# A one-core decoder layer: gated convolution pieces stored from ScalarE's queue one piece later, gates loaded two pieces ahead into five buffers

## The chip, the cores and the metric

The kernel runs on one core of one Trainium2 chip. The metric is the device time of one execution in microseconds; lower is better. The engines are named as in the profile: PE is TensorE (PEld its weight load), DVE is VectorE, ACT is ScalarE, POOL is GpSimd, SP is SyncE. SP, ACT and POOL have queues from which they start DMA transfers; each queue is worked through in its written order, so an instruction that waits holds what stands behind it. SBUF is the on-chip memory, PSUM the accumulators of PE, DRAM the chip's main memory.

## The reference

One decoder layer for a prompt of 2048 tokens and a sample group of 8 x 4 tokens. A normalised input is projected into eleven parts of 512 columns. Four groups of heads are computed from them, each is multiplied by its own gate, and the 2048 columns so made go through `w_out`, a norm and a residual sum:

```python
h = rms_norm(x, pre_g)
z = h @ w_in
y_c, conv_new = conv_branch(ca, cb, conv_hist, w_dw, b_dw, ln_g, ln_b, w_pw, b_pw)
y_p, pool_new = pool_branch(pu, pool_hist, pos, pool_w, pool_scale)
y_s = sb_fn(q, k, v, sb_bias)            # stick-breaking attention
y_m = mem_attend(mq, mk, mv)             # cross attention
mix = concatenate([y_c * silu(cg), y_p * silu(pg), y_s * silu(sg), y_m * silu(mg)])
out = rms_norm(mix @ w_out, post_g)
y = x + out
```

The change touches the end of the convolution branch, `y_c * silu(cg)`. The branch is a gated input, a depthwise convolution of width 31, and then

```python
y = silu(layer_norm(y, ln_g, ln_b))
y = y @ w_pw + b_pw                      # 512 x 512, the "pointwise" product
```

The data are fp32.

## The kernel before

**Stages.** Projections, sample work and the depthwise convolution come first, then the stick-breaking attention of the prompt up to about 1985 us, and then the out stage up to the end. The out stage holds the product `mix @ w_out` and, woven into its first part, the rest of the convolution branch (layer norm, silu, pointwise product, gate). The parts of `mix` go through DRAM: the four groups, as they are finished, are stored to `mixd` (prompt) and `mixs` (sample), and loaded again as the operands of the product.

**Products in fp32.** PE multiplies operands of type fp32r. Each operand is split in two: a rounded copy (`hi`, a cast on ACT) and what that leaves (`lo`, a subtraction on DVE); three matmuls (hi hi, hi lo, lo hi) make one product.

**The product with `w_out`** (L1548 to L1760) is done as seven smaller products over blocks of a 2 x 2 split, in the order 1, 7, 2, 6, 4, 5, 3. Operands are sums and differences of blocks. For a part of `mix`: `out_load` loads `mr` on SP (L1620 to L1644), `out_combine` adds or subtracts two of them on POOL (L1657, L1661) or DVE (L1660), `out_high` casts to `mh` on ACT (L1669), `out_low` makes `ml` on DVE (L1680), and `out_part` runs the matmuls (L1915), four steps of three to a part. Operands are prepared four parts ahead (`AHEAD = 4`). For a weight tile: SP loads `wor` (L1548 to L1560), POOL makes the sum (L1570), ACT casts it to `wohi` (L1576), DVE makes `wolo` (L1581). Sums that a later product needs as well are stored from SP to `wsd` (weights) and `msd` (parts), L1565, and loaded again later.

**The convolution branch here** (`conv_post`, L1388) runs over eight blocks of 256 tokens, named by their first token in buffer names (`cgt512_1` is the gate of block 512, piece 1); the last block also holds the 32 sample tokens. For one block:

- `load` brings `cy` (the convolved input) on SP (L1399), `total` sums its four groups of 128 channels on POOL (L1406), `center` multiplies by a matrix of ones on PE (L1411), subtracts the mean on DVE (L1414), squares on ACT (L1416) and sums on POOL (L1418).
- `scale` does the same product for the variance (`cv`, L1424), then a square root on ACT (L1425, with a table load of its own ahead of it), a reciprocal on DVE (L1426), the affine step on DVE (L1433), the sigmoid on ACT (L1436, with a table load again), the product on DVE (L1440), and the split into `shi` (ACT, L1442) and `slo` (DVE, L1445).
- `point` makes four pieces of 128 output channels. Each has twelve matmuls (L1466) into a PSUM bank `cz`; then DVE adds the bias and multiplies by the gate (L1469), writing over the gate's own tile `cgt`; then SP stores that tile to `mixd` (L1471; in the last block the sample part to `mixs`, L1473). Two steps of the product with `w_out` follow each piece. There are two such PSUM banks, which the `cz` and `cm` tiles take in turn, so a piece's matmuls wait for the gate multiply of an earlier one.
- The gates, silu(cg), were computed earlier and lie in DRAM (`gcd`). `gate(i, co)` loads one piece on SP (L1452) into one of three buffers. The first gate of a block is asked for at the block's start, each other one when the piece before it begins.

The next block's `center` comes ahead of a block's `point`, and the steps of its `scale` after it. The steps of `conv_post` are paced against those of the product (one for every 0.9, `OPACE`), so PE's order is set by the code. DVE, ACT, POOL and SP get theirs from a scheduler, which puts an instruction where it expects its inputs and buffers to be ready. `wq` in the code is SP's queue.

Of the kernel before, what the change touches and what calls it, by code (L numbers as in the profile page):

```python
# [8 lines left out]
F32 = mybir.dt.float32  # L9
# [9 lines left out]
P = 128  # L19
# [30 lines left out]
CB = 256  # L50
# [36 lines left out]
def kernel(  # L87
# [9 lines left out]
    pe, act, dve, pool, sp = nc.tensor, nc.scalar, nc.vector, nc.gpsimd, nc.sync  # L97
    wq = nc.sync
# [22 lines left out]
    gcd = dram.tile([4, P, SEQ + NS], F32, name="gcd")  # L121
# [4 lines left out]
    mixs = dram.tile([4, P, 4, NS], F32, name="mixs")  # L126

    def mix_rows(ct, t0, n):

        return mixd[ct // 4, t0 // P : (t0 + n) // P, :, ct % 4].rearrange("b p t -> p b t")  # L130

    def by_tile(t):
        return t.rearrange("p (b t) -> p b t", t=P)
# [1254 lines left out]
    def conv_post(cp, ps_, weights):  # L1388


        CW = CB + NS
        blocks = [(a, a + CB) for a in range(0, SEQ - CB, CB)] + [(SEQ - CB, SEQ + NS)]
        ys, sums, sqs, split, gates = {}, {}, {}, {}, {}
# [7 lines left out]
        def total(i):  # L1401
            if i < len(blocks):
                a0, N = blocks[i][0], blocks[i][1] - blocks[i][0]
                sums[i] = cp.tile([P, CW], F32, tag="cs", name=f"cs{a0}", bufs=1)[:, :N]
                for c in range(3):
                    pool.tensor_tensor(out=sums[i], in0=sums[i] if c else ys[i][:, 0, :N], in1=ys[i][:, c + 1, :N], op=ALU.add)  # L1406

        def center(i):
            a0, N, y = blocks[i][0], blocks[i][1] - blocks[i][0], ys[i]
            mps = ps_(f"cm{a0}")  # L1410
            pe.matmul(mps[:, :N], lhsT=ones_ln, rhs=sums.pop(i), start=True, stop=True)  # L1411
            sq = []
            for c in range(4):
                dve.tensor_tensor(out=y[:, c, :N], in0=y[:, c, :N], in1=mps[:, :N], op=ALU.subtract)  # L1414
                sq.append(cp.tile([P, CW], F32, tag="csq", name=f"csq{a0}_{c}", bufs=4)[:, :N])
                act.activation(out=sq[c], in_=y[:, c, :N], func=AF.Square)  # L1416
            for a, b in ((0, 1), (2, 3), (0, 2)):
                pool.tensor_tensor(out=sq[a], in0=sq[a], in1=sq[b], op=ALU.add)  # L1418
            sqs[i] = sq[0]

        def scale(i):
            a0, N, y = blocks[i][0], blocks[i][1] - blocks[i][0], ys.pop(i)
            vps = ps_(f"cv{a0}")
            pe.matmul(vps[:, :N], lhsT=ones_ln, rhs=sqs.pop(i), start=True, stop=True)  # L1424
            act.activation(out=vps[:, :N], in_=vps[:, :N], func=AF.Sqrt, bias=eps_t)  # L1425
            dve.reciprocal(out=vps[:, :N], in_=vps[:, :N])  # L1426
            yield
            shi, slo = [cpw.tile([P, 4, CW], F32R, tag=n, name=f"{n}{a0}", bufs=1) for n in ("shi", "slo")]
            for two in ((0, 1), (2, 3)):
                ts = {}  # L1430
                for c in two:
                    t = ps_(f"ct{a0}_{c}")[:, :N]
                    dve.scalar_tensor_tensor(out=t, in0=y[:, c, :N], scalar=par[:, c, CONV_K + 1 : CONV_K + 2],  # L1433
                                             in1=vps[:, :N], op0=ALU.mult, op1=ALU.mult)
                    sg = cp.tile([P, CW], F32, tag="csq", name=f"csg{a0}_{c}", bufs=4)[:, :N]
                    act.activation(out=sg, in_=t, func=AF.Sigmoid, bias=par[:, c, CONV_K + 2 : CONV_K + 3])  # L1436
                    ts[c] = t, sg
                yield
                for c, (t, sg) in ts.items():
                    dve.scalar_tensor_tensor(out=t, in0=t, scalar=par[:, c, CONV_K + 2 : CONV_K + 3], in1=sg,  # L1440
                                             op0=ALU.add, op1=ALU.mult)
                    act.copy(shi[:, c, :N], t)  # L1442
                yield
                for c, (t, _) in ts.items():
                    dve.tensor_tensor(out=slo[:, c, :N], in0=t, in1=shi[:, c, :N].bitcast(F32), op=ALU.subtract)  # L1445
            split[i] = shi, slo
            load(i + 2)

        def gate(i, co):
            a0, a1 = blocks[i]  # L1450
            gates[i, co] = cp.tile([P, CW], F32, tag="cgt", name=f"cgt{a0}_{co}", bufs=3)
            wq.dma_start(gates[i, co][:, : a1 - a0], gcd[co, :, a0:a1])  # L1452

        def point(i):
            a0, a1 = blocks[i]
            N = a1 - a0
            shi, slo = split.pop(i)
            for co in range(4):
                g = gates.pop((i, co))
                if co < 3:  # L1460
                    gate(i, co + 1)
                ps = ps_(f"cz{a0}_{co}")
                n = 0
                for c in range(4):
                    for w, x in ((whi, shi), (whi, slo), (wlo, shi)):
                        pe.matmul(ps[:, :N], lhsT=w[:, c, P * co : P * (co + 1)], rhs=x[:, c, :N], start=n == 0,  # L1466
                                  stop=n == 11)
                        n += 1
                dve.scalar_tensor_tensor(out=g[:, :N], in0=ps[:, :N], scalar=par[:, co, CONV_K + 3 : CONV_K + 4],  # L1469
                                         in1=g[:, :N], op0=ALU.add, op1=ALU.mult)  # L1470
                wq.dma_start(mix_rows(co, a0, CB), by_tile(g[:, :CB]))  # L1471
                if N > CB:
                    wq.dma_start(mixs[0, :, co], g[:, CB:N])  # L1473
                yield
                yield
            flags.add(("conv", i))

        load(0)
# [9 lines left out]
        cpw = weights()  # L1488
# [14 lines left out]
        for _ in range(4):  # L1503
            yield
        for i in range(len(blocks)):
            gate(i, 0)
            side = iter(())
            if i + 1 < len(blocks):
                center(i + 1)
                side = scale(i + 1)  # L1510
            for _ in range(D2):
                yield
            for _ in point(i):
                yield
            total(i + 2)
            for _ in side:
                yield
            for _ in range(D1):
                yield
# [354 lines left out]
    def side_work():  # L1874
        nonlocal opm, conv
        for i, part in enumerate((sample_mem, sample_end)):
            with tc.tile_pool(name=f"sm{i}", bufs=1, side="left", reuse_waits="tile") as sm2:
                yield from part(sm2, side_ps, S)
        opm = ox.enter_context(tc.tile_pool(name="opm", bufs=1, side="left", reuse_waits="tile"))
        yield from out_weights(1, opm, pool)  # L1880
        while (3, 0) not in flags:
            yield
        for x in lead_:
            out_load(x)
            out_combine(x)
            out_high(x)
            out_low(x, pool)
            yield

        while (3, 1) not in flags:  # L1890
            yield
        for x in parts[2 * LEAD : 2 * LEAD + 3]:
            out_load(x)
        cp = cx.enter_context(tc.tile_pool(name="cp", bufs=1, side="left", reuse_waits="tile"))
        conv = conv_post(cp, lambda n: conv_ps[0](n), lambda: cx.enter_context(
            tc.tile_pool(name="cpw", bufs=1, side="left", reuse_waits="tile")))
        while "centered" not in flags:
            next(conv)
            yield
# [130 lines left out]
    for n, x in enumerate(parts):  # L2030
# [8 lines left out]
        prod, i, h = x  # L2039
# [55 lines left out]
```

## Time and profile before

| | |
|---|---|
| median of 3 runs | 2420.67 us (2415.16 to 2429.53) |
| the profiled execution's own time | 2418.47 us |
| its span, first to last instruction | 2416.7 us |
| mean granted PE clock | 0.982 of full speed |
| DVE, ACT, POOL busy over the span | 71%, 46%, 54% |
| gate loads L1452, first to last | 1571.1 to 2208.5 us |
| gate multiplies L1469, first to last | 2012.2 to 2211.0 us |
| stores L1471, first to last | 2012.7 to 2211.5 us |

Profile rows give times in microseconds from the start of the span. A row of the timeline is start, duration, engine, line, operation, output and input, and in square brackets how long the engine had been idle before, with what ended that. A row of a group of instructions ("x46") gives their busy time, the mean duration of one in nanoseconds, the idle time before them in all and what ended it. A row of waits names the engine and line that waited, the engine and line waited for, and then microseconds in all, number of times and the longest. SPq is SP's DMA queue.

### The profile page before, as it was taken

How to read it: one execution, taken by the hardware profiler on the slowest of the kernel's cores; microseconds unless marked ns; L12 is line 12 of the kernel's file. 1: busy time of each engine (PE TensorE's matmuls, PEld its weight loads, DVE VectorE, ACT ScalarE, POOL GpSimd, SP SyncE). 2: the span in 40 equal slices, each digit the busy share in tenths (PEclk: the TensorE clock that was granted, in tenths of full speed). 3: DMA queues.
4: the chain of work that ended last, by engine and by line, in shares of the span. 5: the costliest groups of instructions: out<-in, count | busy, mean ns of one | idle time of the engine just before them, and what ended most of it. 6: DMA issues, size and time to landing. Idle time of an engine off the chain costs nothing. (4 is left out here: it accounts for less than half of the span.)

```text
span 2416.7 us, 42137 instructions
## 1 busy us (share of the span) xinstructions
PE 2285.6 (95%) x15962; PEld 1774.5 (73%) x15962; DVE 1718.3 (71%) x2410; ACT 1117.5 (46%) x1939; POOL 1306.8 (54%) x1333
## 2 busy tenths in 40 slices
PE   7999999999999999999999998899999998989897
PEld 6998978898888777777777776455555556768775
DVE  5333774959757664587877777879798846687998
ACT  5322343242442322124242434788989954443554
POOL 2554544556574555655556564667877755453430
PEclk9999999999999999999999999999999999999998
DMA  5789988887778899987887767834333227887764
GB/s 179 223 260 298 348 290 287 284 272 263 263 254 292 277 344 325 323 287 262 275 270 269 262 218 179 239 79 117 89 88 79 64 64 242 266 272 254 245 234 170
DMA packets 340437, 562.14 MB, mean 233 GB/s; under 512 B 28481, under 2 KB 212929, under 8 KB 323834
## 3 DMA queue, kind: packets, MB, share of 16 engines
q1 hardware_dynamic: 284858, 290.72, 39.2%
q0 software_dynamic: 55376, 268.72, 31.3%
q8 instruction: 126, 2.06, 0.3%
q14 instruction: 77, 0.63, 0.1%
HBM read 469.28 MB, written 90.68 MB: 232 GB/s over the span
## 5 line engine op out<-in xcount | busy, mean ns | idle before, releaser
L959 DVE STREAM_TRANSPOSE T<-kt 128x1024 f32<-128x1024 f32 x256 | 308.9, 1226 | 183.4 <-PE sSA L972 177.2
L926 POOL DMA_INDIRECT vt<-in_cache_v_dram,idv x256 | 251.6, 983 | 242.1 <-PE sO L1011 181.5
L617 DVE SCALAR_TENSOR_TENSOR cacc<-U,par,cacc 128x512 f32<-128x512 f32 x480 | 360.2, 750 | 11.8
L1311 POOL TENSOR_TENSOR be<-be,E 128x512 f32<-128x512 f32 (+2 forms) x320 | 303.8, 957 | 118.4 <-DVE E L1302 52.4
L1302 DVE TENSOR_TENSOR_SCAN E<-gam,cr,ZM 128x513 f32<-128x513 f32 x192 | 232.8, 1262 | 15.1 <-ACT gam L1287 14.2
L926 POOL DMA_INDIRECT kt<-in_cache_k_dram,idk x128 | 126.2, 986 | 201.9 <-DVE T L959 146.8
L1322 PEld LDWEIGHTS AT<-ident,be 128*128 128x128 f32 x1088 | 117.7, 142 | 127.6 <-ACT at L1328 45.4
L1287 ACT ACTIVATE gam<-S,nbias_bc 128x1024 f32<-128x1024 f32 (+1 forms) x160 | 172.6, 1079 | 50.8 <-ACT be L1289 18.9
L1915 PE MATMUL acc<-wohi,mh 128*128 128x512 f32 (+1 forms) x480 | 193.3, 403 | 0.6 <-ACT mh L1669 0.6
L1915 PE MATMUL acc<-wolo,mh 128*128 128x512 f32 (+1 forms) x480 | 189.6, 395 | 0.0
L1915 PE MATMUL acc<-wohi,ml 128*128 128x512 f32 x448 | 178.1, 398 | 11.6 <-DVE ml L1680 11.6
L1282 PE MATMUL S<-kT,Q 128*128 128x512 f32 (+1 forms) x640 | 177.9, 401 | 6.8 <-DMA Q<-qd 2.7
L1289 ACT ACTIVATE be<-S,bias_bc 128x1024 f32<-128x1024 f32 (+1 forms) x160 | 171.6, 1073 | 0.0
L1322 PE MATMUL AT<-ident,be 128*128 128x128 f32 x1088 | 158.1, 284 | 14.1 <-ACT at L1328 4.2
L1338 PE MATMUL av<-at,V 128*64 128x512 f32 (+3 forms) x640 | 153.0, 557 | 1.7 <-DVE sbo L1343 1.7
L972 PE MATMUL sSA<-T,W 128*32 128x128 f32 x4096 | 139.2, 277 | 6.4 <-DVE T L959 5.6
L972 PEld LDWEIGHTS sSA<-T,W 128*32 128x32 f32 x4096 | 104.7, 110 | 43.6 <-issue 35.3
L1680 DVE TENSOR_TENSOR ml<-mr,mh 128x512 fp32r<-128x512 f32 x108 | 98.1, 914 | 38.4 <-ACT mh L1669 38.2
L1282 PEld LDWEIGHTS S<-kT,Q 128*128 128x128 f32 x640 | 107.1, 195 | 23.0 <-ACT be L1289 3.5
L1011 PE MATMUL sO<-vt,saT 128*32 128x512 f32 x1024 | 122.4, 592 | 0.0
L1299 DVE TENSOR_TENSOR_SCAN E<-gam,ZM 128x128 f32<-128x128 f32 (+3 forms) x128 | 96.4, 802 | 30.1 <-ACT gam L1287 25.2
L1328 ACT COPY at<-AT 128x512 f32<-128x512 f32 x192 | 108.9, 655 | 14.4 <-PE AT L1322 14.4
(571 smaller groups left out, 6043.7 us busy)
## 6 DMA issues: line engine op xcount, KB each, us to landing
Q<-qd SPq DMA_DIRECT2D x64, 256.0 KB
mr<-mixd SPq DMA_DIRECT2D x32, 512.0 KB
mr<-mixd SPq DMA_DIRECT2D x48, 256.0 KB
wor<-in_w_out_dram SPq DMA_DIRECT2D x20, 512.0 KB
xtp<-in_x_prompt_dram SPq DMA_DIRECT2D x16, 512.0 KB
kT<-kd SPq DMA_DIRECT2D x64, 128.0 KB
wor<-in_w_out_dram SPq DMA_DIRECT2D x32, 256.0 KB
msd<-mr SPq DMA_DIRECT2D x32, 256.0 KB
```

The lines of the kernel that those rows point to most:

```text
L617: dve.scalar_tensor_tensor(out=ps, in0=U[:, a + k : a + k + H], scalar=wd[:, k : k + 1], in1=ps, op0=ALU.mult, op1=ALU.add)
L926: pool.indirect_dma_start(out=dst, out_offset=None, in_=rows, in_offset=bass.IndirectOffsetOnAxis(ap=idx, axis=0))
L959: dve.transpose(T[:, 2 * hh : 2 * hh + 2].rearrange("p s j t -> p (s j t)"), kt[:, 2 * hh : 2 * hh + 2].rearrange("p s j d -> p (s j d)"))
L972: pe.matmul(sSs[n][32 * g : 32 * g + 32, P * ml : P * (ml + 1)], lhsT=W[:, jj, :], rhs=T[:, :, jj, :], start=i == 0, stop=i == 3, tile_pos ...
L1282: pe.matmul(S[:, j, :w], lhsT=Q[hh][:, x, P * (q2 + j) : P * (q2 + j + 1)], rhs=KT[hp, hh, kc][:, :w], start=x == 0, stop=x == 1)
L1287: act.activation(out=ga[:, :, 512 - w : 512], in_=S[:, :, :w], func=AF.Sigmoid, bias=nbias_bc[:, h : h + 1], scale=-1.0)
L1289: act.activation(out=be[:, :, :w], in_=S[:, :, :w], func=AF.Sigmoid, bias=bias_bc[:, h : h + 1])
L1302: dve.tensor_tensor_scan(out=E[:, j][:, ::-1], data0=ga[:, j][:, ::-1], data1=ZM[:, 0:1].to_broadcast([P, 513]), initial=carry[hh, q2][:, ...
L1311: pool.tensor_tensor(out=be[:, j, :m], in0=be[:, j, :m], in1=E[:, j, 513 - w : 513 - w + m], op=ALU.mult)
L1322: pe.transpose(ap_[:, P * qt : P * (qt + 1)], A[hp, qb, kc, hh, qt][:, P * r : P * (r + 1)], ident)
L1338: pe.matmul(av[64 * hh : 64 * hh + 64, c], lhsT=V[:, 4 * kc + r, 64 * hh : 64 * hh + 64], rhs=ats.pop((hp, qb, kc, r, hh))[:, c], start=dg ...
L1915: pe.matmul(o[:rows], lhsT=m[a][:, k, :rows], rhs=W[prod, 4 * h + k][w], start=not cont and h == k == n == 0, stop=h == 1 and k == 3 and n ...
```

## The change

Gates are taken from one list over all blocks and pieces (`turn`). Each piece now asks for the gates up to two pieces ahead, across the border of a block, and they lie in five buffers of the pool `cpw` instead of three of `cp`. A gated piece is no longer stored at once: it is held, and stored when the next piece's gate multiply has been written (the last piece of a block right behind the block's loop). The store is started from ACT's queue (`act.dma_start`) instead of SP's. The operations and the bytes moved are the same, and PE's order is too.

```diff
@@ -1446,19 +1446,30 @@
             split[i] = shi, slo
             load(i + 2)
 
-        def gate(i, co):
-            a0, a1 = blocks[i]
-            gates[i, co] = cp.tile([P, CW], F32, tag="cgt", name=f"cgt{a0}_{co}", bufs=3)
-            wq.dma_start(gates[i, co][:, : a1 - a0], gcd[co, :, a0:a1])
+        turn = [(i, co) for i in range(len(blocks)) for co in range(4)]
+
+        def gate(upto):
+            while turn and turn[0] <= upto:
+                i, co = turn.pop(0)
+                a0, a1 = blocks[i]
+                gates[i, co] = cpw.tile([P, CW], F32, tag="cgt", name=f"cgt{a0}_{co}", bufs=5)
+                wq.dma_start(gates[i, co][:, : a1 - a0], gcd[co, :, a0:a1])
+
+        def gated(held):
+            while held:
+                a0, N, co, g = held.pop(0)
+                act.dma_start(mix_rows(co, a0, CB), by_tile(g[:, :CB]))
+                if N > CB:
+                    act.dma_start(mixs[0, :, co], g[:, CB:N])
 
         def point(i):
             a0, a1 = blocks[i]
             N = a1 - a0
             shi, slo = split.pop(i)
+            held = []
             for co in range(4):
                 g = gates.pop((i, co))
-                if co < 3:
-                    gate(i, co + 1)
+                gate((i, co + 2) if co < 2 else (i + 1, co - 2))
                 ps = ps_(f"cz{a0}_{co}")
                 n = 0
                 for c in range(4):
@@ -1468,11 +1479,11 @@
                         n += 1
                 dve.scalar_tensor_tensor(out=g[:, :N], in0=ps[:, :N], scalar=par[:, co, CONV_K + 3 : CONV_K + 4],
                                          in1=g[:, :N], op0=ALU.add, op1=ALU.mult)
-                wq.dma_start(mix_rows(co, a0, CB), by_tile(g[:, :CB]))
-                if N > CB:
-                    wq.dma_start(mixs[0, :, co], g[:, CB:N])
-                yield
-                yield
+                gated(held)
+                held.append((a0, N, co, g))
+                yield
+                yield
+            gated(held)
             flags.add(("conv", i))
 
         load(0)
@@ -1503,7 +1514,7 @@
         for _ in range(4):
             yield
         for i in range(len(blocks)):
-            gate(i, 0)
+            gate((i, 1))
             side = iter(())
             if i + 1 < len(blocks):
                 center(i + 1)
```

SP has 36 DMAs fewer and ACT 36 more (32 stores to `mixd`, 4 to `mixs`). In the changed kernel the gate load is L1456, the store L1461, and all later lines stand 11 further down: the gate multiply is L1480, `mh` L1680, `ml` L1691. DVE and SP are also reordered. Three places, with buffer numbers (after the buffer's name stands a number of the tile, which differs between the two kernels):

SP, in block 0, around the store of its last piece, before (`mr7` are loads of parts for product 7, `wsd` stores and `wor7` loads of its weights):

```order
L1627 DMA mr7_0_0_20382<-mixd_63 128x2x512
L1627 DMA mr7_0_1_20440<-mixd_63 128x2x512
L1471 DMA mixd_63<-cgt0_3_20343 128x2x128
L1565 DMA wsd_71<-wor7_4_20218 128x512
L1627 DMA mr7_1_0_20473<-mixd_63 128x2x512
L1565 DMA wsd_71<-wor7_5_20257 128x512
L1548 DMA wor7_6_20307<-in_w_out_dram 128x2x512
L1452 DMA cgt256_0_20483<-gcd_60 128x256
L1548 DMA wor7_7_20395<-in_w_out_dram 128x2x512
```

and now:

```order
L1638 DMA mr7_0_0_20385<-mixd_63 128x2x512
L1638 DMA mr7_0_1_20444<-mixd_63 128x2x512
L1576 DMA wsd_71<-wor7_4_20220 128x512
L1638 DMA mr7_1_0_20477<-mixd_63 128x2x512
L1576 DMA wsd_71<-wor7_5_20259 128x512
L1559 DMA wor7_6_20308<-in_w_out_dram 128x2x512
L1638 DMA mr7_1_1_20515<-mixd_63 128x2x512
L1559 DMA wor7_7_20398<-in_w_out_dram 128x2x512
L1576 DMA wsd_71<-wor7_6_20308 128x512
```

The store of `cgt0_3`, which stood ahead of the two weight stores, is gone, and the gate loads of block 256 have moved.

DVE, in block 1024, from its first gate multiply to its last, before:

```order
L1469 TENSOR_SCALAR cgt1024_0_21297<-cz1024_0_21407,par_117,cgt1024_0_21297 128x256
L1718 TENSOR_TENSOR c11_0_21422<-acc2_0_21349,U2_20000 128x512
L1660 TENSOR_TENSOR mr6_0_1_21343<-mr6_0_1_21343 128x512
L1680 TENSOR_TENSOR ml6_0_0_21433<-mr6_0_0_21285,mh6_0_0_21432 128x512
L1680 TENSOR_TENSOR ml6_0_1_21499<-mr6_0_1_21343,mh6_0_1_21498 128x512
L1581 TENSOR_TENSOR wolo6_6_21457<-wor6_6_21338,wohi6_6_21456 128x512
L1581 TENSOR_TENSOR wolo6_7_21487<-wor6_7_21365,wohi6_7_21486 128x512
L1660 TENSOR_TENSOR mr6_1_0_21372<-mr6_1_0_21372 128x512
L1469 TENSOR_SCALAR cgt1024_1_21405<-cz1024_1_21441,par_117,cgt1024_1_21405 128x256
L1680 TENSOR_TENSOR ml6_1_0_21557<-mr6_1_0_21372,mh6_1_0_21556 128x512
L1660 TENSOR_TENSOR mr6_1_1_21426<-mr6_1_1_21426 128x512
L1469 TENSOR_SCALAR cgt1024_2_21439<-cz1024_2_21471,par_117,cgt1024_2_21439 128x256
```

and now:

```order
L1480 TENSOR_SCALAR cgt1024_0_21145<-cz1024_0_21409,par_117,cgt1024_0_21145 128x256
L1729 TENSOR_TENSOR c11_0_21423<-acc2_0_21351,U2_20000 128x512
L1671 TENSOR_TENSOR mr6_0_1_21345<-mr6_0_1_21345 128x512
L1480 TENSOR_SCALAR cgt1024_1_21173<-cz1024_1_21442,par_117,cgt1024_1_21173 128x256
L1592 TENSOR_TENSOR wolo6_6_21458<-wor6_6_21340,wohi6_6_21457 128x512
L1691 TENSOR_TENSOR ml6_0_0_21434<-mr6_0_0_21289,mh6_0_0_21433 128x512
L1480 TENSOR_SCALAR cgt1024_2_21407<-cz1024_2_21472,par_117,cgt1024_2_21407 128x256
L1592 TENSOR_TENSOR wolo6_7_21488<-wor6_7_21367,wohi6_7_21487 128x512
L1671 TENSOR_TENSOR mr6_1_0_21374<-mr6_1_0_21374 128x512
L1480 TENSOR_SCALAR cgt1024_3_21440<-cz1024_3_21507,par_117,cgt1024_3_21440 128x256
L1691 TENSOR_TENSOR ml6_0_1_21500<-mr6_0_1_21345,mh6_0_1_21499 128x512
```

The second gate multiply stood seven rows behind the first; now two rows stand between them, and the two `ml` and the two `wolo` have moved behind it.

ACT, at the end of block 256 and the square root of block 512, before:

```order
L1693 COPY both1_20584<-acc1_8_20520 32x512
L1669 COPY mh7_1_1_20644<-mr7_1_1_20513 128x512
L1576 COPY wohi2_0_20777<-wor2_0_20650 128x512
L1576 COPY wohi2_1_20804<-wor2_0_20650 128x512
L1669 COPY mh7_2_0_20689<-mr7_2_0_20534 128x512
L1425 ACT_TABLE_LOAD
L1425 ACTIVATE cv512_20659<-cv512_20659,eps_t_94 128x256
```

and now:

```order
L1704 COPY both1_20585<-acc1_8_20522 32x512
L1461 DMA mixd_63<-cgt256_0_20344 128x2x128
L1680 COPY mh7_1_1_20647<-mr7_1_1_20515 128x512
L1461 DMA mixd_63<-cgt256_1_20368 128x2x128
L1461 DMA mixd_63<-cgt256_2_20550 128x2x128
L1587 COPY wohi2_0_20779<-wor2_0_20653 128x512
L1680 COPY mh7_2_0_20693<-mr7_2_0_20536 128x512
L1587 COPY wohi2_1_20806<-wor2_0_20653 128x512
L1461 DMA mixd_63<-cgt256_3_20568 128x2x128
L1425 ACT_TABLE_LOAD
L1425 ACTIVATE cv512_20663<-cv512_20663,eps_t_94 128x256
```

The four stores of block 256 stand between the casts, the last of them right ahead of the table load for the square root.

## The prediction

> **What bounds the kernel now.** I read the page's busy times first, then a table of busy times by windows over the out stage, then who TensorE (PE) waits for there, then the single stalls in PE's timeline, and last, for each stall, the timelines of the engines behind it.
>
> ```profile
> PE 2285.6 (95%) x15962; PEld 1774.5 (73%) x15962; DVE 1718.3 (71%) x2410; ACT 1117.5 (46%) x1939; POOL 1306.8 (54%) x1333
> 2012.00:2044.00 32.00, 22.05 (x106) 17.84 (x107) 17.89 (x36) 14.14 (x30) 18.36 (x17) 0.85 0.75 239
> 2044.00:2076.00 32.00, 28.93 (x154) 24.36 (x152) 21.56 (x37) 14.08 (x27) 16.60 (x15) 0.99 0.85 271
> 2076.00:2108.00 32.00, 30.64 (x159) 25.86 (x160) 21.35 (x39) 15.26 (x28) 13.80 (x13) 1.00 0.80 251
> 2108.00:2145.00 37.00, 27.32 (x118) 21.89 (x117) 25.99 (x42) 14.79 (x29) 22.30 (x17) 0.86 0.86 287
> 2145.00:2220.00 75.00, 74.77 (x391) 63.82 (x390) 63.04 (x104) 35.29 (x71) 26.93 (x21) 1.00 0.80 251
> 2220.00:2416.00 196.00, 169.65 (x723) 132.79 (x721) 169.43 (x276) 94.95 (x242) 61.88 (x40) 0.96 0.66 224
> ```
>
> The window rows give the window and its length, the busy time of PE, PEld, DVE, ACT and POOL, the granted PE clock, the DMA share and GB/s. PE is busy 95% of the span, so time can only be won where PE stands still, or runs at a lower clock after standing still. The changed code runs from 2012 to about 2212. In the 133 us up to 2145 PE is busy 108.9, so 24 us are idle there, at a clock of 0.85 and 0.86 in the two windows with most idle time. From 2145 to 2220 PE is busy 74.77 of 75: nothing to win. After 2220 the changed code is over.
>
> ```profile
> PE cz L1466 <- DVE cgt L1469: 12.0, 4, 5.3
> PE cz L1466 <- ACT shi L1442: 10.2, 2, 8.6
> PE cz L1466 <- DVE slo L1445: 2.4, 5, 1.0
> PE acc L1915 <- DVE ml L1680: 0.2, 1, 0.2
> 2012.70 0.39 PE L1466 MATMUL cz<-shi,pwhi 128*128 128x256 f32 x1 [1.61 <-DVE cgt L1469]
> 2039.69 0.58 PE L1466 MATMUL cz<-shi,pwhi 128*128 128x256 f32 x1 [8.56 <-ACT shi L1442]
> 2077.09 0.39 PE L1466 MATMUL cz<-shi,pwhi 128*128 128x256 f32 x1 [3.14 <-DVE cgt L1469]
> 2121.27 0.39 PE L1466 MATMUL cz<-shi,pwhi 128*128 128x256 f32 x1 [1.66 <-ACT shi L1442]
> 2130.17 0.39 PE L1466 MATMUL cz<-shi,pwhi 128*128 128x256 f32 x1 [2.02 <-DVE cgt L1469]
> 2138.48 0.58 PE L1466 MATMUL cz<-shi,pwhi 128*128 128x256 f32 x1 [5.25 <-DVE cgt L1469]
> ```
>
> The waits of PE from 2012 to 2220 (us, times, longest) are 24.8 us in all, and 22.2 of them are on two things: the gate multiply that frees the PSUM bank of two pieces back (`cgt` L1469), and the split of the convolution's input (`shi` L1442). The six stalls shown are these 22.2. They are what the change can win.
>
> **Part 1: the stores leave SP's queue.** SP issues in order, so a store that waits for its gate multiply holds every load behind it.
>
> ```profile
> SPq L1471 <- DVE cgt L1469: 49.0, 25, 7.1
> 2016.39 1.06 SPq L1627 DMA_DIRECT2D mr<-mixd  x2
> 2023.20 0.36 SPq L1471 DMA_DIRECT2D mixd<-cgt  x1
> 2025.71 0.46 SPq L1565 DMA_DIRECT2D wsd<-wor  x1
> 2030.36 0.37 SPq L1548 DMA_DIRECT2D wor<-in_w_out_dram  x1
> 2018.79 2.61 POOL L1570 TENSOR_TENSOR wor<-wor 128x512 f32<-128x512 f32 x2 [2.85 <-DMA wor<-in_w_out_dram]
> 2036.11 1.26 POOL L1570 TENSOR_TENSOR wor<-wor 128x512 f32<-128x512 f32 x1 [2.47 <-DMA wor<-in_w_out_dram]
> 2037.41 0.62 ACT L1576 CAST wohi<-wor 128x512 fp32r<-128x512 f32 x1 [2.11 <-POOL wor L1570]
> 2037.93 0.83 ACT L1436 ACTIVATE csg<-ct,par 128x256 f32<-128x256 f32 x2
> ```
>
> SP spends 49 us in such waits from 2012 to 2220. One of them reaches PE. SP stands from 2017.45 (2016.39 + 1.06) until block 0's last gate is done, and issues its store at 2023.20. The second weight store behind it goes at 2025.71, though POOL had its data at 2021.40 (2018.79 + 2.61). That store frees the buffer of the weight load at 2030.36, whose sum POOL begins at 2036.11; ACT's cast of it waits until 2037.41, and the sigmoids, and so `shi`, stand behind the cast. This chain ends in the 8.56 us stall. Without the store on SP the weight store can go at 2021.40, 4.3 us earlier, and the rest with it. In the new ACT order the two sigmoids also stand ahead of that cast, which is worth up to another 0.83 + 0.62. The bounds are 0, if the loads land no sooner because the DMA engines are loaded at 0.75, and the whole 8.56. I take 5.5, 4.3 and most of 1.45, the sum of the rows.
>
> ```profile
> 2042.60 0.41 PE L1466 MATMUL cz<-slo,pwhi 128*128 128x256 f32 x1
> 2046.28 0.28 PE L1466 MATMUL cz<-slo,pwhi 128*128 128x256 f32 x1
> ```
>
> Three us after the 8.56 us stall a matmul still takes 0.41, and 3.7 us later the same one takes 0.28. The window from 2012 to 2044 lost 3.3 us so (22.05 busy at 0.85); a shorter stall takes some of that along: 2.0 (0 to 3.3; for the other stalls I count none).
>
> **Part 2: the gate multiplies move ahead on DVE.** With gates loaded two pieces ahead the scheduler sets the multiplies earlier, and that bears on three stalls.
>
> ```profile
> 2011.55 0.69 DVE L1581 TENSOR_TENSOR wolo<-wor,wohi 128x512 fp32r<-128x512 f32 x1 [1.83 <-ACT wohi L1576]
> 2012.16 0.48 DVE L1469 SCALAR_TENSOR_TENSOR cgt<-cz,par,cgt 128x256 f32<-128x256 f32 x1
> 2075.55 1.09 DVE L1680 TENSOR_TENSOR ml<-mr,mh 128x512 fp32r<-128x512 f32 x1 [1.81 <-ACT mh L1669]
> 2076.57 0.86 DVE L1469 SCALAR_TENSOR_TENSOR cgt<-cz,par,cgt 128x256 f32<-128x256 f32 x2
> 2129.65 0.47 DVE L1469 SCALAR_TENSOR_TENSOR cgt<-cz,par,cgt 128x256 f32<-128x256 f32 x1
> 2131.33 2.38 DVE L1680 TENSOR_TENSOR ml<-mr,mh 128x512 fp32r<-128x512 f32 x2
> 2135.52 1.92 DVE L1581 TENSOR_TENSOR wolo<-wor,wohi 128x512 fp32r<-128x512 f32 x2 [1.80 <-ACT wohi L1576]
> 2137.95 0.48 DVE L1469 SCALAR_TENSOR_TENSOR cgt<-cz,par,cgt 128x256 f32<-128x256 f32 x1
> ```
>
> - Block 0: the first gate stood behind `wolo`, which had waited 1.83 for ACT; now it stands ahead of it. Bounds 0 and the stall, 1.6; I take 1.2, since an `ml` now stands ahead in its place.
> - Block 1024: between its first gate (2129.65) and its second (2137.95) stood two `ml`, two `wolo` with a wait of 1.80, and three other rows. Now two rows stand between, and the stall of 5.25 loses its cause. Bounds 0 and 5.25; I take 4.5, for the `ml` that moves behind is needed by PE only after the next piece. The stall of 2.02 there, on the first gate, stays.
> - Block 512: the second gate moves ahead of two `wolo`, but stays behind the `ml` that waited for ACT at 2075.55. Bounds 0 and 3.1; I take 1.5.
>
> The multiplies displaced from the front run in DVE's idle time: in these windows DVE is busy 17.9 to 26.0 of 32 to 37.
>
> **Part 3: what ACT pays.**
>
> ```profile
> L1471 SPq DMA_DIRECT2D mixd<-cgt x32: 359/371/487, 2012.7 to 2211.5; - x32
> L1425 ACT ACT_TABLE_LOAD x7 | 9.0, 1283 | 0.1
> L1425 ACT ACTIVATE cv<-cv,eps_t 128x256 f32<-128x256 f32 (+1 forms) x7 | 3.2, 452 | 12.8 <-PE cv L1424 12.8
> L1669 ACT CAST mh<-mr 128x512 fp32r<-128x512 f32 (+1 forms) x46 | 27.6, 606 | 49.5 <-POOL mr L1657 23.0 <-PE acc L1915 9.5 <-issue 8.5
> ```
>
> 32 stores of 0.37 and the last block's four extra ones make about 13 us of issuing on ACT. ACT is idle more than half of each window, and in front of its `mh` casts alone it waits 49.5 us, so I count 0 for the issuing itself; uncovered it would be the 13. The fourth store of each block is a case of its own. It stands right ahead of the table load for the square root, which before ran in the 12.8 us (1.8 a block) that the root waited for PE. Now table load and store (1.28 + 0.37 = 1.65) follow the gate. Bounds 0 and 1.65 in each of seven blocks, 11.6; I take half of it in the four blocks whose `shi` or `slo` releases a PE wait: 3.3. The new wait in front of these stores has `mh`, `wohi` and the root behind it; being a piece late covers three stores of four. The gate loads stay on SP; each now also waits for ACT's store five buffers back, with `mr` loads behind it. These loads run four parts ahead of PE, so I count 0; uncovered, a gate load would wait like a store did, 2 us on average.
>
> **The sum**, against the profiled execution's own 2418.47 us (span 2416.7, 2.2 under the median 2420.67 and inside the 2415.16 to 2429.53 of the runs): 5.5 + 2.0 + 1.2 + 4.5 + 1.5 = 14.7 won, 3.3 lost, so 11.4 less: 2407. Its own bounds: a quarter of the 14.7 won and 3.3 lost give 2418; all five terms at their upper ends, 8.6 + 3.3 + 1.6 + 5.2 + 3.1 = 21.8, and nothing lost give 2397.
>
> **The rivals.**
>
> *More is won.* All gate and `shi` stalls go, 12.0 + 10.2, with the 2.0 of clock, and the root's table load stays covered: 2394. For it: the stalls are chained, each late `shi` sets the next block late. Against: 2.02 of them hangs on a block's first gate, which does not move, and 1.66 on a block's input, for which the change does nothing directly.
>
> *Nothing is won: the DMA engines set the pace.* The same bytes move, and in the windows with stalls the DMA share is 0.75 to 0.86. If the loads are late for lack of transfer rate, those issued 4.3 us earlier land no earlier, each stall comes back under another name, and the time is 2418. Against: from 2145 to 2220 the share is 0.80 and PE is not held at all. The Trainium skill ("DMA: Bandwidth & Descriptors", "Issuing engines are not separate DMA queues") says that DMAs of all issuing engines share the same 16 engines, and that a second issuer saves only the sequencer's time. By that rule alone this rival would be the answer; the 49.0 us row shows that here the sequencer's time is a wait, not an issue, so the trace bears it out in part.
>
> *Slower: ACT is held by its stores.* SP's stores waited 49.0 / 25 = 1.96 us on average. If the fourth store of a block waits that long on ACT, it holds the table load too: 1.96 + 0.37 + 1.28 = 3.6 a block, 25.3 over seven, all on the way to `shi`; the 7.5 of part 1 is lost with it. 2418.5 - 7.2 + 25.3 = 2437. For it: the chain through the root has 1.8 a block to spare, and the 10.2 us row shows that PE already waits for it. It decides once store, wait and table load exceed 1.8 a block by more than the 14.7 won. Against: before, much of the SP waiting came from DVE orders that change.
>
> *The change does nothing*, because the scheduler leaves the order alone: excluded by the orders shown.
>
> **How the numbers follow.** Forecast case 0.46, more 0.17, nothing 0.15, slower 0.22. About 0.5%, 12 us, is what a measurement of this kernel tells from no change; against the median that is under 2408.6 or over 2432.8. Of the forecast case 0.28 lies under it, with 0.17 from the larger gain: faster 0.45. Same: 0.18 + 0.15 = 0.33. Slower 0.22. The likeliest case alone spans 2397 to 2418; the range reaches from 2394 to 2434, leaving out most of the slow case and little of the fast.
>
> **What would show it.** Right: no PE stall over 4 us near 2039 or 2138, the weight store near 2021, the SP row of 49.0 gone, a clock over 0.9 in both windows now at 0.85. Wrong: ACT rows with long waits at the stores ahead of the table load, new PE stalls on `shi` at the start of blocks 512 to 1792, or SP waits of several us at gate loads.

## The result and the profile after

The changed kernel is slower: 2430.24 us median (2420.62 to 2438.08) against 2422.55 us (2415.16 to 2430.28) for the kernel before, ratio 1.0028 (95% interval 1.0018 to 1.0037), so about 7 us lost where 11 were to be won. That is less than the 0.5% that the prediction took for its mark, but the interval leaves out 1. The profiled execution took 2422.3 us, its span is 2420.6 against 2416.7; it is the second shortest of the 22, and its first gate multiply starts 2.7 us earlier than that of the kernel before (2009.5 against 2012.2).

First the windows of the changed kernel, in the columns of the prediction (busy time of PE, PEld, DVE, ACT, POOL, then the granted clock and the DMA share):

```profile
2012.00:2044.00 32.00, 25.15 (x126) 20.05 (x125) 18.42 (x36) 14.87 (x30) 18.84 (x16) 0.89 0.85 279
2044.00:2076.00 32.00, 27.68 (x136) 23.33 (x135) 21.63 (x38) 14.44 (x28) 14.79 (x12) 0.89 0.84 273
2076.00:2108.00 32.00, 31.89 (x166) 26.91 (x164) 23.88 (x39) 17.02 (x32) 18.29 (x16) 1.00 0.96 315
2108.00:2145.00 37.00, 33.06 (x162) 27.53 (x161) 34.94 (x59) 19.54 (x42) 18.74 (x15) 0.95 0.86 285
2145.00:2220.00 75.00, 72.17 (x365) 60.80 (x364) 55.58 (x90) 29.60 (x59) 27.08 (x23) 0.98 0.72 228
2220.00:2418.00 198.00, 166.00 (x695) 129.01 (x693) 166.43 (x270) 93.30 (x239) 60.46 (x38) 0.93 0.62 213
```

Up to 2145 us PE is now busy 117.8 of 133 us, not 108.9: the gain that was looked for is there. From 2145 to 2220 it has idle time that it had not before. Its waits from 2012 to 2220, and the longest of them in its timeline:

```profile
PE cz L1477 <- ACT shi L1442: 11.4, 4, 4.0
PE cz L1477 <- DVE cgt L1480: 3.4, 2, 2.8
PE cz L1477 <- DVE slo L1445: 1.9, 5, 0.9
PE acc L1926 <- DVE ml L1691: 1.1, 1, 1.1
2036.41 0.58 PE L1477 MATMUL cz<-shi,pwhi 128*128 128x256 f32 x1 [3.94 <-ACT shi L1442]
2065.35 0.58 PE L1477 MATMUL cz<-shi,pwhi 128*128 128x256 f32 x1 [3.97 <-ACT shi L1442]
2124.29 0.39 PE L1477 MATMUL cz<-shi,pwhi 128*128 128x256 f32 x1 [2.80 <-DVE cgt L1480]
2171.65 0.38 PE L1477 MATMUL cz<-shi,pwhi 128*128 128x256 f32 x1 [2.01 <-ACT shi L1442]
```

The waits fell from 24.8 to 17.8 us. Those on the gate multiply went from 12.0 to 3.4; those on `shi` stayed, 11.4 against 10.2, now at block 256 (twice), block 512 and block 1536.

PE's order is the same in both kernels, so its matmuls can be paired one by one. The changed kernel's lead over the kernel before, worked out so from the two traces (times are those of the kernel before):

```
at us        1990  2045  2080  2120  2140  2160  2186  2220  2270  2320  2360  2380   end
lead of PE   +1.9  +4.0  +2.0  +3.7 +10.5 +11.7  +6.4  +6.5  +3.8  +0.8  +1.6  +0.5  -3.9
```

Out of 1.9 us before the stage grew 11.7 by 2160. Nearly half of it went at block 1536 (2165 to 2186). All the rest, and 3.9 us more, went behind the last gate multiply, in a stretch whose code the change does not touch. There the two profiles differ so (waits of DVE from 2215 us on and one of SP, then the window from the last gate multiply to PE's last matmul and, roughly, the one behind it; the first fence is of the changed kernel, the second of the kernel before):

```profile
DVE acc L1738 <- DMA gpost<-in_post_g_dram: 2.7, 1, 2.7
DVE wolo L1592 <- ACT wohi L1587: 8.9, 6, 2.5
DVE ml L1691 <- ACT mh L1680: 5.0, 8, 1.9
SPq L1631 <- DVE oss L1764: 4.5, 1, 4.5
2204.20:2398.50 194.30, 181.80 (x763) 141.90 (x762) 160.56 (x254) 90.99 (x225) 65.82 (x42) 0.97 0.67 225
2398.00:2421.00 23.00, 0.51 (x3) 0.07 (x1) 14.40 (x29) 7.82 (x24) 0.00 (x0) 0.58 0.29 114
```

```profile
DVE wolo L1581 <- ACT wohi L1576: 6.0, 5, 1.8
DVE ml L1680 <- ACT mh L1669: 2.8, 3, 1.7
DVE mh L1680 <- ACT mh L1669: 2.9, 1, 2.9
2211.50:2399.00 187.50, 178.10 (x760) 139.67 (x758) 162.07 (x260) 93.15 (x233) 64.61 (x42) 0.99 0.71 237
2398.00:2417.00 19.00, 1.05 (x5) 0.52 (x3) 11.66 (x23) 5.69 (x19) 0.00 (x0) 0.63 0.27 107
```

The whole stretch takes 11.2 us longer than before: 6.8 of them up to PE's last matmul (194.3 against 187.5 us) and 4.4 behind it. In the first part PE's granted clock is 0.97 instead of 0.99, and PE waits 12.5 us instead of 9.4, all but 0.5 of it for DVE. DVE, which in the kernel before is busy 169 of 196 us there, waits longer for `wohi` (8.9 us against 6.0) and once 2.7 us for the norm's weights `gpost`; for `mh` it waits no longer in these rows (5.0 against 2.8 and 2.9). When PE has ended, 14.4 us of closing norm work are still before DVE, where it was 11.7. The order of the instructions differs too: in the changed kernel rows that serve later products (`ml`) or add up their results (`acc`) stand a few rows further ahead of the norm (`oss`, `oxt`). Whether that is the cause is tried in e5 to e7. A piece of DVE's order near the end, - before, + changed:

```
 TENSOR_SCALAR oxt8<-oxt8,oss8,gfin
-TENSOR_TENSOR ml5_6_0<-mr4_6_0,mh5_6_0
+TENSOR_TENSOR ml3_6_0<-mr3_6_0,mh3_6_0
 TENSOR_TENSOR oss11<-ssk
-TENSOR_TENSOR acc3_5<-acc3_5,U2
+TENSOR_TENSOR acc4_6<-acc4_6,U3
 RECIPROCAL oss11<-oss11
-TENSOR_TENSOR ml5_6_1<-mr4_6_1,mh5_6_1
+TENSOR_TENSOR ml3_6_1<-mr3_6_1,mh3_6_1
 TENSOR_SCALAR oxt11<-acc4_5,oss11,oxt11
```

### The profile page after: what moved, and what is told of

Its sections match the earlier page's. It is cut to its first block, busy times and chain, and to the rows that moved or that the text cites. A ratio compares the mean times of both kernels' runs of the same rounds, so it can differ in the third digit from the quotient of the medians.

```text
span 2420.6 us, 42138 instructions
## 1 busy us (share of the span) xinstructions
PE 2285.3 (94%) x15962; PEld 1771.2 (73%) x15962; DVE 1723.4 (71%) x2410; ACT 1116.4 (46%) x1939; POOL 1304.8 (54%) x1333
## 5 line engine op out<-in xcount | busy, mean ns | idle before, releaser
L926 POOL DMA_INDIRECT kt<-in_cache_k_dram,idk x128 | 125.7, 982 | 208.6 <-DVE T L959 154.6
L1926 PE MATMUL acc<-wohi,mh 128*128 128x512 f32 (+1 forms) x480 | 195.7, 408 | 4.5 <-DVE mh L1691 3.2
L1691 DVE TENSOR_TENSOR ml<-mr,mh 128x512 fp32r<-128x512 f32 x108 | 97.6, 912 | 34.1 <-ACT mh L1680 33.6
L1328 ACT COPY at<-AT 128x512 f32<-128x512 f32 x192 | 109.0, 657 | 14.4 <-PE AT L1322 14.4
```

The costliest lines, as they stand in the source:

```text
L926: pool.indirect_dma_start(out=dst, out_offset=None, in_=rows, in_offset=bass.IndirectOffsetOnAxis(ap=idx, axis=0))
L1926: pe.matmul(o[:rows], lhsT=m[a][:, k, :rows], rhs=W[prod, 4 * h + k][w], start=not cont and h == k == n == 0, stop=h == 1 and k == 3 and n ...
```

## The experiments

Each ratio is to the kernel before, run in the same session, with its 95% interval. Two times from each profile tell the two parts of the stage apart: from the first to the last gate multiply ("with convolution"), and from there to the end of the span ("behind it"). Theories A to E are stated in the expectations below.

| run | ratio | with convolution, us | behind it, us |
|---|---|---|---|
| before | 1 | 198.8 | 205.7 |
| changed | 1.0028 (1.0018 to 1.0037) | 194.2 | 216.9 |
| e1 stores only | 1.0005 (0.9992 to 1.0018) | 194.3 | 210.0 |
| e2 gates only | 1.0041 (1.0027 to 1.0056) | 199.8 | 219.1 |
| e3 stores late, from SP | 1.0051 (1.0035 to 1.0067) | 199.5 | 216.0 |
| e4 last store behind the root | 1.0027 (1.0013 to 1.0041) | 195.0 | 214.6 |
| e5 changed, old order behind | 0.9977 (0.9962 to 0.9992) | 193.0 | 204.5 |
| e6 changed, old order all through | 0.9984 (0.9970 to 0.9998) | 194.9 | 205.9 |
| e7 before, new order behind | 1.0052 (1.0031 to 1.0072) | 197.5 | 218.1 |
| e8 as e5, on DVE alone | 0.9993 (0.9981 to 1.0006) | 195.7 | 208.6 |
| e9 as e5, on the others alone | 1.0002 (0.9989 to 1.0015) | 196.3 | 211.3 |
| e10 e2, old order behind | 1.0004 (0.9993 to 1.0015) | 200.3 | 207.4 |
| e11 e1, old order behind | 0.9993 (0.9981 to 1.0005) | 191.9 | 207.9 |
| e12 buffers from the other pool | 1.0040 (1.0026 to 1.0054) | 196.8 | 216.6 |

Profiles of kernels that have the same order on DVE in a part still differ there by up to some 4 us: with convolution 193.0 to 196.3 (changed, e5, e8, e9) and 191.9 and 194.3 (e11, e1); behind it 204.5 to 207.9 with the old order (before, e5, e6, e10, e11) and 214.6 to 219.1 with the new one (changed, e2, e3, e4, e7). Each of these is one execution; the ratios rest on 6 to 22 of each kernel.

**The halves (e1 to e4).** The first suspect was ACT. In the changed kernel it stands long in front of the table load of the square root, behind which the rest of the layer norm is queued:

```profile
ACT L1425 <- DVE cgt L1480: 7.7, 3, 4.7
ACT L1425 <- DMA mixd<-cgt: 7.5, 2, 4.8
2154.42 2.74 ACTq L1461 DMA_DIRECT2D mixd<-cgt  x2
2157.20 1.28 ACT L1425 ACT_TABLE_LOAD   x1 [4.83 <-DMA mixd<-cgt]
```

e1 takes the kernel before and moves the stores alone:

```diff
-                wq.dma_start(mix_rows(co, a0, CB), by_tile(g[:, :CB]))
...
+                gated(held)
+                held.append((a0, N, co, g))
...
+            gated(held)
```

> The stores go from ScalarE's queue one piece later, the gates are loaded as before (one piece ahead, three buffers). Theory A: the loss comes from ScalarE, whose table load for the square root stands behind a block's last store (15.2 us of waits there in the changed kernel), so this half alone is slower than before by 0.2 to 0.5% (ratio 1.002 to 1.005). Theory B: whatever is won or lost up to block 1792 is evened out in the last 200 us, where VectorE is the bound and has its own order; ratio 0.998 to 1.003, with a lead or lag of TensorE at 2140 us that is not found again at the end.

e2 takes the gates alone (the changed kernel with the stores as before):

```diff
-                gated(held)
-                held.append((a0, N, co, g))
+                wq.dma_start(mix_rows(co, a0, CB), by_tile(g[:, :CB]))
...
-            gated(held)
...
```

> The gates are loaded two pieces ahead into five buffers, the stores stay on SyncE's queue, right behind their multiply. Theory A: the multiplies move ahead on VectorE without a cost on ScalarE, so it is faster than before, ratio 0.996 to 0.998. Theory B: ratio 0.998 to 1.003, any lead at 2140 us is gone at the end.

e3 leaves the stores a piece late, but on SP's queue:

```diff
-                act.dma_start(mix_rows(co, a0, CB), by_tile(g[:, :CB]))
+                wq.dma_start(mix_rows(co, a0, CB), by_tile(g[:, :CB]))
...
```

> As the changed kernel, but the stores, one piece late, are started from SyncE's queue. Theory A: no wait in front of ScalarE's table load, and SyncE's waits for the gate multiplies well under the 49 us of before; ratio 0.995 to 0.998. Theory B: ratio 0.998 to 1.003.

e4 puts a block's last store behind the next square root, by an edge that sets the order on ACT and no wait:

```diff
...
-            gated(held)
-            flags.add(("conv", i))
+            kept.append((i, held))
...
+            more = next(side, 0)
+            with tc.issue_after(roots[-1]) if i + 1 < len(blocks) else ExitStack():
+                gated(kept[0][1])
+            flags.add(("conv", kept.pop()[0]))
...
```

> As the changed kernel, but a block's last store is put behind the next block's square root on ScalarE, so that the table load stands ahead of it as before. Theory A: the 15.2 us of waits in front of the table load go, TensorE keeps most of its lead of 11.8 us at block 1024; ratio to before 0.996 to 0.999, some 10 us under the changed kernel. Theory B: like the changed kernel, 1.001 to 1.004.

Theory A fell on all four. The stores alone lose nothing (1.0005), the gates alone lose 0.4%, the late stores from SP 0.5%, and to move the last store from in front of the table load, which cuts ACT's waits there from 15.2 to 5.0 us, changes nothing (1.0027 against 1.0028). Theory B had the place, the last 200 us, but not that all variants come out even there. The table shows what goes together. The stores from ACT take some 4 us off the part with convolution (e1, e4, changed), the gates nothing (e2, e3), and the later runs agree: 191.9 to 196.3 us in the eight profiles with the stores on ACT, 196.8 to 200.3 in the six with them on SP; and each kernel with the gates ahead needs 215 to 219 us behind it. In e2, e4 and the changed kernel DVE's order there is the same row for row, with or without the stores on ACT; its rows lie 2.1 places on average from where they stood before. In e1, whose gates stay in the old pool, they lie 0.6 from there.

**The order behind the last gate multiply (e5 to e7).** A list of all instructions of an engine, in the order that the scheduler gave another kernel, is laid down by edges between neighbours that set the order and no wait:

```diff
+KEPT = {'DVE': [...], 'Activation': [...], 'Pool': [...], 'SP': [...]}
...
+    for eng, ranks in KEPT.items():
+        L = [i for i in tc.nc.cur_bb.bb.instructions
...
+        for a, b in zip(ranks, ranks[1:]):
+            tc.add_manual_dep(L[b], L[a].name, mb.DependencyInfo(mb.DependencyClass.NoSync,
+                              mb.DependencyReason.DATA), reason="order")
```

e5 lays the old order on the changed kernel, behind the last gate multiply (281 instructions on DVE, 185 on ACT, 47 on POOL, 125 on SP):

> The changed kernel, but behind the last gate multiply every instruction of VectorE, ScalarE, GpSimd and SyncE's queue stands in the order that the scheduler gave it in the kernel before (edges that set the order and no wait); up to there it keeps its own order. Theory C (the loss is the order of the last 200 us, which the scheduler sets anew when the gate multiplies move): the 4.4 us that the end falls behind TensorE's last products go, and with them part of the loss; ratio to before 0.998 to 1.001. Theory D (the loss comes with the transfers themselves, the gates loaded earlier or the stores from ScalarE's queue): as the changed kernel, 1.002 to 1.004.

e6 does so from block 0 on, for all but the gate loads and the stores:

> The changed kernel, but from block 0's first gate multiply on all instructions of VectorE, ScalarE, GpSimd and SyncE's queue other than the gate loads and the stores stand in the order of the kernel before. What is left of the change is that the stores go from ScalarE's queue one piece later, and that the gates are loaded earlier. Theory C: no loss, ratio 0.997 to 1.001. Theory D: 1.002 to 1.004.

e7 lays the new order on the kernel before:

> The kernel before, but behind the last gate multiply all instructions of VectorE, ScalarE, GpSimd and SyncE's queue stand in the order of the changed kernel. Nothing else of the change is in it. Theory C: slower than before by most of the change's loss, ratio 1.0015 to 1.003, with the end some 4 us further behind TensorE's last products. Theory D: no change, 0.999 to 1.001.

Theory C had the direction right each time, but e5 and e7 went further than its ranges (0.998 to 1.001 and 1.0015 to 1.003). With the old order the changed code is faster than the kernel before (0.9977), and the kernel before, with nothing but the new order of its last 218 us, is slower (1.0052). e6 comes out near e5 (0.9984, the intervals overlap). The profiles show it in place: the gate multiplies, first and last start, the span, and waits from 2215 us on, of e5 and then of e7 (the kernel before has 9.4 us for `ml` and no wait for `gpost`).

```profile
L1482 DVE SCALAR_TENSOR_TENSOR cgt<-cz,par,cgt x32: 469/484/520, 2017.0 to 2210.0; 128x256 f32<-128x256 f32 x28, 128x288 f32<-128x288 f32 x4
core 0: 2414.5 us, clock 0.982
PE acc L1928 <- DVE ml L1693: 7.7, 6, 3.2
```

```profile
L1471 DVE SCALAR_TENSOR_TENSOR cgt<-cz,par,cgt x32: 468/478/521, 2014.4 to 2211.9; 128x256 f32<-128x256 f32 x28, 128x288 f32<-128x288 f32 x4
core 0: 2430.0 us, clock 0.980
PE acc L1917 <- DVE ml L1682: 11.0, 7, 4.0
DVE wolo L1583 <- ACT wohi L1578: 10.3, 6, 2.9
DVE acc L1729 <- DMA gpost<-in_post_g_dram: 3.1, 1, 3.1
SPq L1622 <- DVE oss L1755: 5.0, 1, 5.0
```

The wait for `gpost`, which neither the kernel before nor e5 has, comes along with the new order. Its chain can be followed in the changed kernel, in the timelines of SP and DVE:

```profile
2269.02 1.08 SPq L1576 DMA_DIRECT2D msd<-mr  x2
2274.58 0.52 SPq L1631 DMA_DIRECT2D mr<-mixs  x1
2275.15 0.62 SPq L2048 DMA_DIRECT2D gpost<-in_post_g_dram  x1
2274.47 0.15 DVE L1764 TENSOR_TENSOR oss<-ssk 128x1 f32<-128x1 f32 x1
2275.98 0.69 DVE L1691 TENSOR_TENSOR ml<-mr,mh 128x512 fp32r<-128x512 f32 x1
2279.36 1.90 DVE L1738 TENSOR_TENSOR acc<-acc,gpost 128x512 f32<-128x512 f32 x3 [2.68 <-DMA gpost<-in_post_g_dram]
```

SP stands from 2270.1 to 2274.6 with a load that waits for DVE to have got past a row of the norm; the load of `gpost` is queued behind it and is not there when DVE's order asks for it. DVE waits 2.7 us, and in this stretch PE waits for DVE in 12.0 of its 12.5 us of waits.

**Which engine's order (e8, e9), and what the halves are worth with equal ends (e10, e11).** e8 keeps of e5's lists only DVE's, e9 all but DVE's; e10 and e11 are e2 and e1 with all of e5's lists.

> As the changed kernel with the old order behind the last gate multiply, but on VectorE alone. Theory C1 (it is VectorE's order: products' low halves ahead of the closing norm): all of the recovery, ratio to before 0.996 to 1.000. Rival C2 (it is SyncE's and ScalarE's order: loads and casts that come late): none of it, 1.001 to 1.004.

> The complement: the old order behind the last gate multiply on ScalarE, GpSimd and SyncE's queue, VectorE left in the changed kernel's order. Theory C1: still slow, 1.001 to 1.004. Rival C2: recovered, 0.996 to 1.000.

> Gates two pieces ahead, stores on SyncE's queue as before, and the old order behind the last gate multiply on all four. With the last stretch equal, what the gates alone are worth shows. Prediction's part 2 (multiplies moved ahead on VectorE, 7.2 us): ratio 0.996 to 0.998. If the gates alone win nothing while stores hold SyncE's queue: 0.999 to 1.001.

> Stores from ScalarE's queue one piece later, gates as before, and the old order behind the last gate multiply. Prediction's part 1 with part 3 (7.5 us won, 3.3 lost): ratio 0.997 to 0.999. If the stores alone win nothing: 0.999 to 1.001.

e8 (0.9993) and e9 (1.0002) both recover most of the loss and, by their medians, neither as much as e5, so C1 and C2 are not told apart. Nor do the two runs separate the engines: in e9, with the other engines' lists laid down, the scheduler moved DVE's rows by 1.6 places on average from the changed kernel's order, to 1.2 from the old one; in e8 SP's rows came back to 0.1 places from their old order. The engines' orders hang together. Of e10 and e11, the gates alone win nothing (1.0004), where part 2 had 0.996 to 0.998; the stores alone 0.9993, with an interval that takes in 1 and also reaches the 0.997 to 0.999 expected. e10's waits of PE, from 2012 to 2212, show what became of part 2:

```profile
PE cz L1471 <- ACT shi L1444: 13.2, 6, 4.6
PE acc L1920 <- DVE ml L1685: 4.7, 3, 3.6
PE cz L1471 <- DVE slo L1447: 2.1, 5, 0.9
PE cz L1471 <- DVE cgt L1474: 0.9, 2, 0.7
```

The wait for the gate multiply is gone, 12.0 to 0.9. The `ml` that had to make room for it are waited for now, 0.2 to 4.7, and `shi` takes 3.0 more.

**Why the order changed (e12).** The diff moves the gate buffers from the pool `cp` to `cpw`. In the kernel before, the program makes the splits of product 4's weights wait for the last gate stores, because they lie in the memory that the gate buffers had; in the changed kernel it is the load and the sum of the second of these weights that wait for gate multiplies and stores. e12 is the kernel before with one word changed:

```diff
-            gates[i, co] = cp.tile([P, CW], F32, tag="cgt", name=f"cgt{a0}_{co}", bufs=3)
+            gates[i, co] = cpw.tile([P, CW], F32, tag="cgt", name=f"cgt{a0}_{co}", bufs=3)
```

> The kernel before with one word changed: the three gate buffers are taken from the pool cpw, as in the changed kernel, instead of cp. Gates are still loaded one piece ahead and stored at once from SyncE's queue; the order up to the last gate multiply hardly moves, the order behind it becomes nearly that of the changed kernel. Theory E (the loss comes in through the place of the buffers, by the order that the scheduler then gives the last 200 us): slower than before, ratio 1.002 to 1.005, TensorE level with before up to 2200 us and some 8 to 13 us behind at the end. Rival (it takes the look-ahead or the earlier multiplies to lose the time): 0.999 to 1.001.

Theory E held: 1.0040. DVE's rows behind the last gate multiply lie 0.4 places on average from the changed kernel's order and 2.3 from that of the kernel before. The gate multiplies, the span and the wait for `gpost`:

```profile
L1469 DVE SCALAR_TENSOR_TENSOR cgt<-cz,par,cgt x32: 467/479/518, 2015.3 to 2212.1; 128x256 f32<-128x256 f32 x28, 128x288 f32<-128x288 f32 x4
core 0: 2428.7 us, clock 0.980
DVE acc L1727 <- DMA gpost<-in_post_g_dram: 3.3, 1, 3.3
```

With gates one piece ahead and stores at once from SP, the part with convolution takes 196.8 us, where the same order but for a few rows took 198.8 and 197.5 (before, e7), and the rest 216.6. Paired with the kernel before, PE lags 5.0 us at 1990, 1.1 at 2220 and 7.2 at 2380, and the end 12.0.

## Why the prediction was wrong, point by point

**"After 2220 the changed code is over."** This step failed. The prediction costed the last stretch at nothing, because no line of it changes. The change moved buffers to another pool, that moved which later tiles wait for them, and the scheduler set the order of the last stretch anew on DVE, ACT and SP, and hardly on POOL. It costs 11.2 us in the profiles (216.9 against 205.7). e12 shows that the place of the buffers is enough for it, e7 that the order is, and e5 that without it the change wins. That 2430 lies inside the range all the same is luck: the range reached so far for the sake of the slower rival, whose mechanism e4 does not bear out.

**Part 1 (5.5 and 2.0 won).** The chain was there, its size was wrong. In the changed kernel the second weight store goes out as soon as POOL's sum is done, and the load, the sigmoids and the end of the stall follow earlier too:

```profile
2022.44 0.33 SPq L1576 DMA_DIRECT2D wsd<-wor  x1
2027.99 0.37 SPq L1559 DMA_DIRECT2D wor<-in_w_out_dram  x1
2034.02 0.84 ACT L1436 ACTIVATE csg<-ct,par 128x256 f32<-128x256 f32 x2
```

These stood at 2025.71, 2030.36 and 2037.93, and the stall ends at 2036.41 instead of 2039.69, 3.3 us earlier. But PE was 1.9 ahead when it came into the stage, so by 2045 it had won 2.1 us, where the sum has 5.5 + 2.0 + 1.2 for block 0. The stall itself shrank further, from 8.56 to 3.94, and the clock of its window rose from 0.85 to 0.89; yet part of that is only that PE came to it later, after waits of 1.48 and 0.86 for the same block. In e6, where all but the gate loads and the stores keep their old order, PE's waits from 2012 to 2212 are

```profile
PE cz L1479 <- DVE cgt L1482: 11.6, 4, 5.2
PE cz L1479 <- ACT shi L1444: 7.7, 3, 5.5
```

so the waits on `shi` fall by 2.5, the longest from 8.6 to 5.5, and the waits on the gate multiply stay. In the same pairing of matmuls e6 wins 2.2 us by 2045.

**Part 3 (3.3 lost).** The price was put in the wrong place: ACT does wait, 15.2 us in front of the table load, but e4 took two thirds of that away and won nothing. That 7.5 won and 3.3 lost make 4.2, and that e1's part with convolution is 4.5 us shorter (194.3 against 198.8), is a coincidence: e1's waits from 2012 to 2220 are

```profile
PE cz L1474 <- ACT shi L1442: 12.4, 7, 3.5
PE cz L1474 <- DVE cgt L1477: 3.6, 2, 2.8
```

It waits longer for `shi` than the kernel before, 12.4 against 10.2, and less for the gate multiply, 3.6 against 12.0, which the prediction had given to the gates (part 2).

**SP's queue.** The Trainium skill ("DMA: Bandwidth & Descriptors", "Issuing engines are not separate DMA queues") says that a second issuer saves only the sequencer's time to start a DMA. By that alone nothing would have been won, and the prediction's rival had 2418 for it. No run here bears that out for the part with convolution: it is shorter in every profile with the stores on ACT than in any with them on SP, by some 4 us on average, also in e6 with the old order (194.9). SP's waits did not become fewer for it: from 2012 to 2220 they add up to 125.7 us, before to 108.1. The 49.0 us at the stores are gone, but 17.7 us stand now at the gate loads, which the prediction had at 0 and which wait for ACT's stores:

```profile
SPq L1456 <- DMA mixd<-cgt: 17.7, 7, 5.8
```

**Part 2 (7.2 won).** This was wrong. Its three stalls did go; of the waits on the gate multiply, 12.0 us, the changed kernel has 3.4 and e10 0.9. But the gates alone shorten nothing (199.8 and 200.3 us against 198.8), since `shi` and `ml` come late in their place; and the stores alone remove as much of these waits. Paired with the kernel before, from 2115 to 2140 (block 1024, where the sum has 4.5) the changed kernel wins 8.0 us, e1 8.1 and e2 7.1. In all three two rows stand between the first and the second gate multiply of that block. Either half of the change moves the multiplies, so their gains do not add.

**The lead of 11.7 us at 2160**, 9.8 of it won in the stage, comes near the 11.4 predicted, but by luck, since it was won at another place: of the 9.8, 2.1 stood at 2045 and 0.1 at 2080, and 8.0 came at block 1024. It is nearly halved at block 1536. There DVE stood 3.98 us with a row for product 6 that waits for a load, and the reciprocal of that block's layer norm stood behind it:

```profile
2161.28 0.69 DVE L1671 TENSOR_TENSOR mr<-mr 128x512 f32<-128x512 f32 x1 [3.98 <-DMA mr<-msd]
```

In the kernel before the same row stands 21 us later. PE then waits 2.01 us for `shi` (2171.65), and its granted clock from 2170 to 2175 is 0.79. The loss of half the lead there is read from the traces; no run takes that wait away.

**The rivals.** None of them named what happened. The slower one had ACT held by its stores, and e4 speaks against it, though 5.0 us of these waits are left there. The prediction's three signs of being wrong did come (15.2 us on ACT, new stalls on `shi` at blocks 512 and 1536, 17.7 us at the gate loads), but they do not account for the loss: e5 has them too (14.2 us on ACT, 22.7 at the gate loads) and is faster than the kernel before. "Nothing is won" had the DMA engines as the bound; shares of 0.84 to 0.96 did not keep PE from getting ahead.

**Left open.** Which of the moved rows behind the last gate multiply cost how much, beyond the 2.7 us at `gpost`, why the scheduler's new order follows from the other place in memory, which was read from the program and not tried by itself, and why the stores alone move the gate multiplies on DVE.

## What to carry to other kernels

Where a scheduler sets the order, compare the order of the whole program, not of the part that is edited: a buffer that moves to another pool changes what waits for its memory later on, and with that the order of code that nobody touched. A loss that shows in such a place can be tried by laying the old order on the new code; here that turned 0.28% slower into 0.23% faster (e5, the fastest of all that ran). Where two halves of a change each remove the same wait, do not add their gains. And a wait of the bound engine that is removed by letting its releaser go first is worth only what the displaced work can spare.

## What was not expected of the hardware

The profiles reach the out stage at different times, though the programs hardly differ up to there: the first gate multiply starts between 2007.6 (e10) and 2023.3 us (e2). That is more than any difference looked for here, so stretches within a profile, from one fixed instruction to another, told more than its span.
